# Two parts of the FFN's Down as seven half-width products, with the next part's first features ahead of them

## The chip, the cores and the metric

The kernel runs on one core of a Trainium2 chip. The time is device time in microseconds (us) of one execution. TensorE (PE in the profile; its weight loads are PEld) multiplies, VectorE (DVE), ScalarE (ACT) and GpSimd (POOL) work on tiles, and SyncE (SP) issues DMA transfers; POOL and ACT can issue transfers too. PE writes to PSUM, eight banks of 128 x 512 float32; the other tiles lie in SBUF, 128 partitions wide.

## The reference

A two-layer trunk over 512 positions and 1024 features. Each layer is

```python
x = x + 0.5 * swiglu(rms_norm(x, ffn1_norm[l]), ffn1_w_gate[l], ffn1_w_up[l], ffn1_w_down[l])
...     # mixer: causal convolution beside differential attention with a relative-position bias
x = x + jnp.concatenate([conv_out, diff_out], axis=-1) @ w_out[l]
x = x + 0.5 * swiglu(rms_norm(x, ffn2_norm[l]), ffn2_w_gate[l], ffn2_w_up[l], ffn2_w_down[l])

def swiglu(h, w_gate, w_up, w_down):
    return (jax.nn.silu(h @ w_gate) * (h @ w_up)) @ w_down
```

with 2816 hidden features in each FFN, all in float32. There are four FFNs in all, two in each layer, and they are most of the time.

## The kernel before, in words

**Layout.** Features are on the partitions and positions along the free dimension: `x` is eight tiles of 128 x 512. The 2816 hidden features are 22 feature tiles. Every float32 operand is split in a high part (ACT, a copy to float32r) and a low part (DVE, the difference), by `parts_of` (L95 to L97) for weights and by other lines for activations; `mm3` (L160 to L166) multiplies with three matmuls: high x high, high x low, low x high.

**One FFN** (`ffn`, from L382) goes through its 22 feature tiles in three parts, (0 to 5), (6 to 13), (14 to 21). For each part it makes the gated features, and then adds the part's share of the Down product to `x`.

- Part one is plain: per feature tile, Gate and Up each take 8 input tiles x 3 matmuls of 512 columns. The first two feature tiles go through `first_products`, beside which the row norm is worked out (`rows_rstd`, `spread`). At the start of the kernel the weights of the first tile, `lead`, are loaded in halves.
- From tile 6 on, Gate and Up of one feature tile are made together by `seven`: the two outputs, the two halves of the contraction and the two halves of the columns form a 2 x 2 by 2 x 2 block product, which takes seven block products in place of eight. Each is 4 input tiles x 3 matmuls of 256 columns, so a feature tile takes 84 of them. Its activations are sums and differences of the normalised input, made once per FFN by `Halves` and put in place by `settle`. Its weights are sums of blocks, made for each feature tile by `sums` (L123): SP loads the raw tiles, POOL issues one transfer that adds onto a loaded tile (L140), POOL adds twice (L145, L146), and ACT and DVE split the results. `rest`, the last of the seven products and the gating, is carried out inside the next tile's `seven`, by `finish`.
- Down is plain in all three parts (L429 to L444): for each of the eight outputs as many feature tiles as the part has, 3 matmuls of 512 each into `ps_d`, weights by `gather` in chunks of eight blocks; DVE then adds half the sum to `x` (L442). After the last part, `after(m)` prepares `x` tile m for the next stage (`Prep.tile`), or writes it out.

**Buffers.** Raw, high and low weight tiles lie in rings: `wraw` has five slots of 1024 columns, `whi` and `wlo` four, the half-size rings two. A transfer waits until its slot has been read for the last time. PSUM banks rotate in three pairs (`turn_tag`, `pair_banks`).

**Order.** The program is traced once; a planner then fixes the order of the instructions on each engine ahead of time, by priority in program order and its own model of times. Each engine and each DMA queue works its list in that order, so whatever stands behind a waiting instruction waits too. Matmuls marked `keep_in_program_order` are not moved against each other: here the first matmul of each of the seven products.

**The mixer** adds the position bias to the scores in `softmaxes` (L681). The bias table, 128 x 4 x 512, is made once by `make_bias` during the first FFN and kept in SBUF (`bias`, loaded by POOL's queue).

## Time and profile before

| | |
|---|---|
| median of three runs | 1805.25 us (1803.75 to 1805.65) |
| the profiled execution | 1805.29 us, span 1803.5 us |
| granted TensorE clock | full (1.0) |
| PE busy, matmuls | 1786.9 us, 10692 |
| DVE, ACT, POOL busy | 1207.3, 884.2, 616.7 us |
| matmuls of `seven` (L352), 256 columns | 5376 |
| matmuls of Down (`ps_d`), 512 columns | 2112 |
| DMA | 227 MB, 126 GB/s over the span |

How to read the lines of the profile: a group of instructions stands with its line in the kernel, its engine, the operation and output<-input. In the chain that ended last each line is the start in us, the time in us and what ran. In the timeline each line is the start, the time from there to the end, and the instruction; what stands in brackets is the engine's idle time before it and what ended that. SPq is SP's DMA queue. Matmuls are pipelined: one of 512 columns shows 0.39 us, while the next starts 0.23 us after it.

### The profile page before, as it was taken

The page shows a single profiled execution, that of the slowest core. Times are in us where ns is not written, and L with a number is a line of the kernel's source. Part 1 is how long each engine was busy: PE and PEld are TensorE (multiplying, and loading weights), DVE is VectorE, ACT ScalarE, POOL GpSimd, SP SyncE. Part 2 cuts the span into 40 slices and gives each one's busy share as a digit, 9 for nine tenths or more (in the row PEclk, how much of TensorE's full clock was granted, in tenths as well). Part 3 has the DMA queues.
Part 4 walks back from the last instruction along what each step waited for, and adds up shares of the span by engine and source line. Part 5 has one row for each costly group of instructions (what it writes and reads, how often), then busy time and mean ns, then how long its engine had stood idle before and what let it go on. Part 6 is the DMA issues. An engine that isn't in the chain of part 4 may idle for free.

```text
span 1803.5 us, 27857 instructions
## 1 busy us (share of the span) xinstructions
PE 1786.9 (99%) x10692; PEld 1584.1 (88%) x10692; DVE 1207.3 (67%) x1852; ACT 884.2 (49%) x1448; POOL 616.7 (34%) x432
## 2 busy tenths in 40 slices
PE   8999999999999999999999999999999999999999
PEld 6799899888778889899888998998887888998997
DVE  7857557568867857557576684665788587574662
ACT  5536346445854436346434462554558354463551
POOL 3035123269942024133110341322797320231320
PEclk9999999999999999999999999999999999999999
DMA  6357456322212347546433474653231133574561
GB/s 219 125 149 197 135 144 179 115 89 90 75 41 88 107 116 183 155 126 182 126 93 103 127 201 108 167 172 106 71 107 57 47 103 97 146 178 133 154 171 51
DMA packets 104853, 227.00 MB, mean 126 GB/s; under 512 B 11527, under 2 KB 29094, under 8 KB 104720
## 3 DMA queue, kind: packets, MB, share of 16 engines
q1 hardware_dynamic: 85536, 188.78, 32.3%
q0 software_dynamic: 19040, 36.36, 11.7%
q8 instruction: 83, 1.36, 0.3%
q14 instruction: 50, 0.41, 0.1%
q10 hardware_dynamic: 144, 0.08, 0.0%
HBM read 223.07 MB, written 3.42 MB: 126 GB/s over the span
## 4 chain that ended last, share of the span: by engine, by line
PE 95%; DVE 2%; ACT 1%; issue 1%; DMA 0%; SPq 0%; ACTq 0%; DVEq 0%
PE ps_pair L352 36%; PE ps_d L166 9%; PE ps_d L162 9%; PE ps_d L165 9%; PE ps_pair L166 6%; PE ps_pair L165 6%; PE ps_pair L162 6%; PE ps_pair L559 2%; PE ps_pair L560 2%; PE ps_pair L561 2%; PE ps_out L165 1%; PE ps_out L162 1%; PE ps_sc L677 1%; PE ps_out L166 1%; DVE actl L248 1%; PE ps_v L591 1%
## 5 line engine op out<-in xcount | busy, mean ns | idle before, releaser
L96 ACT ACTIVATE whi<-wraw 128x1024 fp32r<-128x1024 f32 (+1 forms) x578 | 459.0, 817 | 648.9 <-PE ps_d L165 226.1
L97 DVE TENSOR_TENSOR wlo<-wraw,whi 128x512 fp32r<-128x512 f32 (+1 forms) x534 | 513.6, 984 | 184.1 <-ACT whi L96 179.2
L352 PE MATMUL ps_pair<-acth,wlo 128*128 128x256 f32 x1024 | 289.8, 283 | 0.0
L352 PE MATMUL ps_pair<-actl,whi 128*128 128x256 f32 x1024 | 289.8, 283 | 0.0
L352 PE MATMUL ps_pair<-acth,whi 128*128 128x256 f32 x1024 | 289.7, 283 | 0.0
L165 PE MATMUL ps_d<-hl,whi 128*128 128x512 f32 x704 | 274.0, 389 | 0.0
L166 PE MATMUL ps_d<-hh,wlo 128*128 128x512 f32 x704 | 272.7, 389 | 0.0
L162 PE MATMUL ps_d<-hh,whi 128*128 128x512 f32 x704 | 268.9, 389 | 0.0
L140 POOL DMA_DIRECT2D wraw<-in_gu x64 | 77.2, 1207 | 452.6 <-DMA wraw<-in_gu 210.8
L352 PE MATMUL ps_pair<-th,wlo 128*128 128x256 f32 x768 | 217.3, 283 | 0.0
L352 PE MATMUL ps_pair<-tl,whi 128*128 128x256 f32 x768 | 217.2, 283 | 0.0
L352 PE MATMUL ps_pair<-th,whi 128*128 128x256 f32 x768 | 217.2, 283 | 0.0
L162 PE MATMUL ps_pair<-acth,whi 128*128 128x512 f32 x512 | 200.6, 395 | 5.5 <-ACT whi L96 5.5
L165 PE MATMUL ps_pair<-actl,whi 128*128 128x512 f32 x512 | 201.1, 393 | 2.0 <-DVE actl L248 1.6
L166 PE MATMUL ps_pair<-acth,wlo 128*128 128x512 f32 x512 | 200.5, 392 | 0.6 <-DVE wlo L97 0.6
L442 DVE SCALAR_TENSOR_TENSOR x<-ps_d,x 128x512 f32<-128x512 f32 x96 | 65.0, 689 | 197.3 <-PE ps_d L166 197.3
L352 PEld LDWEIGHTS ps_pair<-acth,whi 128*128 128x128 f32 x1024 | 196.6, 192 | 0.3
L352 PEld LDWEIGHTS ps_pair<-actl,whi 128*128 128x128 f32 x1024 | 196.6, 192 | 0.3
L352 PEld LDWEIGHTS ps_pair<-acth,wlo 128*128 128x128 f32 x1024 | 196.6, 192 | 0.0
L145 POOL TENSOR_TENSOR wraw<-wraw 128x512 f32<-128x512 f32 x64 | 87.8, 1373 | 304.3 <-DMA wraw<-in_gu 220.1
L165 PEld LDWEIGHTS ps_d<-hl,whi 128*128 128x128 f32 x704 | 132.2, 188 | 27.0
L166 PEld LDWEIGHTS ps_d<-hh,wlo 128*128 128x128 f32 x704 | 132.2, 188 | 27.0
(174 smaller groups left out, 3306.4 us busy)
## 6 DMA issues: line engine op xcount, KB each, us to landing
wraw<-in_gu SPq DMA_DIRECT2D x110, 512.0 KB, 3.6
wraw<-in_gu SPq DMA_DIRECT2D x196, 256.0 KB, 3.9
wraw<-in_gu POOLq DMA_DIRECT2D x64, 512.0 KB, 5.6
wraw<-in_wqkv SPq DMA_DIRECT2D x24, 512.0 KB, 3.5
wraw<-in_dn SPq DMA_DIRECT2D x52, 192.0 KB, 3.0
wraw<-in_wag SPq DMA_DIRECT2D x16, 512.0 KB, 3.5
wraw<-in_wout SPq DMA_DIRECT2D x16, 512.0 KB, 3.5
wraw<-in_dn SPq DMA_DIRECT2D x24, 320.0 KB, 3.4
```

The lines of the kernel that those rows point to most:

```text
L96: S.activation(hi, raw, AF.Copy)
L97: (eng or V).tensor_tensor(out=lo, in0=raw, in1=f32(hi), op=ALU.subtract)
L140: nc.gpsimd.dma_start(two.rearrange("p (b c) -> p b c", b=2), u[:, h[0]].unsqueeze(1).broadcast_to([P, 2, 512]), accum_op=ALU.add)
L145: G.tensor_tensor(more[:, h[0]], two[:, h[1]], whole[:, h[0]], op=ALU.add)
L162: first = T.matmul(ps, wh, xh, start=start, stop=False)
L165: T.matmul(ps, wh, xl, start=False, stop=False)
L166: T.matmul(ps, wl, xh, start=False, stop=stop)
L352: mm = T.matmul(ps, l, r, start=first and i == j == 0, stop=False, skip_group_check=True)
L442: V.scalar_tensor_tensor(x[:, m, :], ps, 0.5, x[:, m, :], op0=ALU.mult, op1=ALU.add)
L559: T.matmul(ps[n], xh[:, t], wh, start=k == 0, stop=False)
L560: T.matmul(ps[n], xh[:, t], wl, start=False, stop=False)
L561: T.matmul(ps[n], xl[:, t], wh, start=False, stop=k == KT - 1)
```

## The change

**Parts.** There are now four parts, of 6, 6, 6 and 4 feature tiles. The first and the last are as before (class `Kept`: plain Down). The two in the middle are `Paired`: their Down is made by `seven` too, for two outputs at a time, with the contraction of six tiles in two halves of three, and the columns in two halves. The class makes the sums and differences of two gated tiles, `kk` and `kk + 3`, as soon as both are there, so its features are made in the order 0, 3, 1, 4, 2, 5. The weights come from `sums`, now with blocks of 384 columns (`n`) and with sources that can lie across two stored chunks (`blocks_of`), in which case a load is two transfers. What follows the products is in the new classes `Gate` (for Gate and Up, as before but for `second`) and `Update` (for Down: it adds to `x`, with one addition on POOL, `kept`).

**Order.** After a paired part's last feature, the first feature of the next part is put ahead of the Down products. `late` now runs on from features to Down and on into the next part.

**Start.** The weights of the first two feature tiles are loaded and split in halves, all first halves ahead of the second ones, with the `x` tiles between; `lead_products` runs the two tiles' Gate and Up side by side over the input tiles, and the norm's `spread` moves into the third tile's second product.

**Bias.** `make_bias` stops at the copy in DRAM; each mixer loads the table from there through SP's queue into its own memory. Some scratch tiles (`make_scalars`, `Halves`) use other buffers.

```diff
-PARTS = ((0, 6), (6, 8), (14, 8))
+PARTS = (
+    ((0, 1, 2, 3, 4, 11), False), (tuple(range(5, 11)), True), (tuple(range(12, 18)), True), (tuple(range(18, 22)), False),
+)
...
+    def blocks_of(src, half, b0):
+        def get(a, b):
+            got, at = [], a
+            while at < b:
+                n, c = divmod(b0 * P + at, 1024)
+                w = min(b - at, 1024 - c)
+                got.append((at - a, at - a + w, src[half, n][:, c : c + w]))
+                at += w
+            return got
+        return get
...
+        load(whole[:, both], g, 0)
         two = ring("wraw")
+        load(two[:, h[0]], g, 0)
+        load(two[:, h[1]], u, n)
+        u2 = ring("wraw2", 512)[:, :n]
+        load(u2, u, n)
+        for c0, c1, ap in u(0, n):
+            nc.gpsimd.dma_start(
+                two[:, both].rearrange("p (b c) -> p b c", b=2)[:, :, c0:c1],
+                ap.unsqueeze(1).broadcast_to([P, 2, c1 - c0]), accum_op=ALU.add,
+            )
...
-    nc.scalar.dma_start(pars[0], par[0])
-    nc.sync.dma_start(x[:, 0, :], xt[0])
-    lead = [chunk(gu1[0, 0, i], cuts=2) for i in range(2)]
-    for k in range(1, KT):
-        nc.sync.dma_start(x[:, k, :], xt[k])
-    nc.gpsimd.dma_start(pars[1], par[1])
+    for l in range(DEPTH):
+        nc.scalar.dma_start(pars[l], par[l])
+    lead = [[ring("wraw"), ring("whi"), ring("wlo")] for _ in range(4)]
+    for half in range(2):
+        h, kk = slice(half * 512, (half + 1) * 512), range(half * KT // 2, (half + 1) * KT // 2)
+        nc.sync.dma_start(x[:, kk[0], :], xt[kk[0]])
+        for n, (raw, hi, lo) in enumerate(lead):
+            nc.sync.dma_start(raw[:, h], gu1[0, n // 2, n % 2][:, h])
+            parts_of(raw[:, h], hi[:, h], lo[:, h])
+        for k in kk[1:]:
+            nc.sync.dma_start(x[:, k, :], xt[k])
...
+    def lead_products(pr, w, ps):
+        for k in range(KT):
+            for n in range(2):
+                for i in range(2):
+                    mm3(ps[n][i], wpart(w[n][i], k), pr[k], k == 0, k == KT - 1)
+        return rows_rstd(pr.s, DM, pin=True)[0]
...
+    class Paired:
+        BLOCKS = {"b11": 0, "t1": 1, "t2": 2, "t3": 3, "t4": 4, "b21": 5, "b22": 6}
+        def __init__(self, fp, many, ahead):
+            self.fp, self.half = fp, many // 2
+            self.made, self.t = {}, {}
+            self.order = [kk + n for kk in range(self.half) for n in (0, self.half)]
+        def place(self, kk, bank):
+            if kk >= self.half:
+                return bank
+            self.t[kk] = self.fp.tile([P, 5, HS], F32, tag="ht", name="ht")
+            return self.t[kk][:, :2].rearrange("p n c -> p (n c)")
+        def took(self, kk, us):
+            if kk < self.half:
+                return
+            kk -= self.half
+            t = self.t[kk]
+            us = us.rearrange("p (n c) -> p n c", n=2)
+            hi, lo = (self.fp.tile([P, 7, HS], F32R, tag=f"hw{n}", name="hw") for n in (kk, self.half + kk))
+            S.activation(hi[:, 5:], us, AF.Copy)
+            V.tensor_tensor(t[:, 3], us[:, 1], t[:, 1], op=ALU.subtract)
+            V.tensor_tensor(t[:, 1], t[:, 0], t[:, 1], op=ALU.subtract)
+            V.scalar_tensor_tensor(t[:, 2], us[:, 1], -1.0, t[:, 1], op0=ALU.mult, op1=ALU.subtract)
+            V.scalar_tensor_tensor(t[:, 4], us[:, 0], -1.0, t[:, 2], op0=ALU.mult, op1=ALU.subtract)
+            S.activation(hi[:, :5], t, AF.Copy)
+            V.tensor_tensor(lo[:, 5:], us, f32(hi[:, 5:]), op=ALU.subtract)
+            V.tensor_tensor(lo[:, :5], t, f32(hi[:, :5]), op=ALU.subtract)
+            self.made[kk] = hi, lo
...
+    class Gate:
+        scale = 1.0
...
+        def first(self, two, keep):
+            V.tensor_tensor(two, two, keep[:, 0::2], op=ALU.add)
+            S.activation(keep[:, 0::2], two, AF.Silu)
+        def second(self, a, keep, bank):
+            V.tensor_tensor(keep[:, 1::2], a, keep[:, 1::2], op=ALU.add)
+            us = self.part.place(self.kk, bank)
+            V.scalar_tensor_tensor(
+                us.rearrange("p (n c) -> p n c", n=2), keep[:, 1::2], -1.0, keep[:, 0::2], op0=ALU.mult, op1=ALU.mult
+            )
+            self.part.took(self.kk, us)
+    class Update:
+        scale = -0.5
+        def __init__(self, m):
+            self.x = [x[:, m + i].rearrange("p (n c) -> p n c", n=2) for i in range(2)]
+        def kept(self, keep):
+            G.tensor_tensor(self.x[1], self.x[1], keep[:, 1::2], op=ALU.add)
+        def first(self, two, keep):
+            V.scalar_tensor_tensor(keep[:, 0::2], two, 0.5, keep[:, 0::2], op0=ALU.mult, op1=ALU.subtract)
+            V.tensor_tensor(self.x[0], self.x[0], keep[:, 0::2], op=ALU.add)
+        def second(self, a, keep, bank):
+            V.scalar_tensor_tensor(self.x[1], a, -0.5, self.x[1], op0=ALU.mult, op1=ALU.add)
...
+                if paired:
+                    if n + 1 < len(PARTS):
+                        pair(n + 1, 0, False)
+                    half, f0 = divmod(fs[0], HALF)
+                    for m in range(0, KT, 2):
+                        g, u = (blocks_of(dn, half, (m + i) * HALF + f0) for i in range(2))
+                        w = sums(g, u, part.half * P)
+                        end = n + 1 == len(PARTS) and m + 2 == KT
+                        late.append(seven(part, part.half, w, pair_banks(next(turn)), fp, finish, end, Update(m)))
...
-        skew = bass.AP(d2.tensor, d2.offset + P - 1, [[RLEN - 1, P], [P * RLEN, HEADS], [1, SEQ]])
-        nc.gpsimd.dma_start(bias, skew)
+        skew.append(bass.AP(d2.tensor, d2.offset + P - 1, [[RLEN - 1, P], [P * RLEN, HEADS], [1, SEQ]]))
...
+            bias = mp.tile([P, HEADS, SEQ], F32, tag="bias", name="bias")
+            nc.sync.dma_start(bias, skew[0])
+            row["bias"] = bias
```

## The prediction

> **What bounds the kernel now.** First the page: busy time by engine, and the chain that ended last.

> ```profile
> PE 1786.9 (99%) x10692; PEld 1584.1 (88%) x10692; DVE 1207.3 (67%) x1852; ACT 884.2 (49%) x1448; POOL 616.7 (34%) x432
> ...
> PE 95%; DVE 2%; ACT 1%; issue 1%; DMA 0%; SPq 0%; ACTq 0%; DVEq 0%
> ```

> TensorE is the bound, but overlapping matmuls make 99% say nothing of their pace. That is read from the chain in order of time:

> ```profile
> 20.06 0.50 PE ps_pair L165
> 21.71 2.25 DVE wlo L97
> 24.00 0.50 PE ps_pair L166
> ...
> 92.28 0.68 PE ps_d L162 x3
> 113.59 76.31 PE ps_pair L352 x636
> ```

> A 512-column matmul takes 0.68 / 3 = 0.2267 us, a 256-column one 76.31 / 636 = 0.1200 us. From 24 us on each FFN is gapless at these two paces, so fewer columns on PE is time, if the weights keep coming. How near they come to being late is in the timeline of one gate/up pair (seven x 12 matmuls, 10.08 us; this one begins at 142.2 us):

> ```profile
> 140.58 1.21 POOL L140 DMA_DIRECT2D wraw<-in_gu  x1
> 146.39 1.30 POOL L145 TENSOR_TENSOR wraw<-wraw 128x512 f32<-128x512 f32 x1 [4.61 <-DMA wraw<-in_gu]
> 147.77 2.33 POOL L146 TENSOR_TENSOR wraw<-wraw 128x512 f32<-128x512 f32 x1
> 151.17 1.20 POOL L140 DMA_DIRECT2D wraw<-in_gu  x1 [1.07 <-DVE wlo L97]
> ...
> 144.72 0.42 SPq L136 DMA_DIRECT2D wraw<-in_gu  x1
> ...
> 147.71 1.23 DVE L97 TENSOR_TENSOR wlo<-wraw,whi 128x1024 fp32r<-128x1024 f32 x1
> ...
> 149.50 1.16 ACT L96 ACTIVATE whi<-wraw 128x512 fp32r<-128x512 f32 x2 [0.72 <-PE ps_pair L352]
> ```

> POOL issues the adding transfer, waits until it has landed (5.8 us from issue), adds twice (3.7 us), and only then issues the next: a round of 9.5 us in a period of 10.08. The sums are there at 146.39 and ACT takes them at 149.50, so they are about 3.1 us ahead (2.6 to 3.1 in this stage). The POOL add beside a DVE split took 2.33 us, an undisturbed one 1.30 (at 101.38 us).

> **The sum is made against** the profiled execution, 1805.29 us (span 1803.5, 1.8 around it), 0.04 from the median of the three runs, 1805.25.

> **Products, -19.2 us.** Of the 22 feature tiles of an FFN, 12 get their Down as seven products. For two outputs and six tiles, 2 x 6 x 3 = 36 matmuls of 512 (8.16 us) become 7 x 3 x 3 = 63 of 256 (7.56 us): 0.60 saved. Four output pairs, two parts, four FFNs: 32 x 0.60 = 19.2. Gate and Up keep their counts (six plain pairs, sixteen by seven). The pace of 0.1200 holds with a fresh weight load per matmul, so the added loads are in it.

> **Start, -4 us.** The first matmul begins at 5.53 us; the six plain pairs end at 80.73. Going back from there, four pairs are 192 x 0.2267 = 43.5 us and the bias and spread matmuls between them 1.9, so two pairs and the row sums end at 35.3. Gapless from 5.53 they would end at 5.53 + 96 x 0.2267 + 0.35 = 27.6: 7.6 us are lost, because a feature tile gives PE 6 matmuls (1.36 us) while ACT needs 0.71 + 0.62 for it and DVE 1.1 to 1.6. With both pairs interleaved a tile gives 12 (2.72 us), longer than either. What stays: four first halves must be in place for the first tile. The first transfers come in at 8.04 (ACT's wait), ACT then needs some 0.6 for each, so the first 12 matmuls end near 10.2 instead of 8.25: 2 us. The lead also holds all four slots of whi and wlo, and the third pair's chunk is split (1.06 + 1.3) only behind a first output with nine matmuls left (2.0): about 0.5. Gain 7.6 - 2.5 = 5; I take 4, since DVE shares those microseconds with POOL's row sums. Bounds: -5.5, and +1 if the third pair waits for a whole split. The late normaliser (spread in the third pair's second product) is ready about 4 us after the row sums, used after 7.5; three pairs to gate at once instead of two keep DVE, already full from 40 to 60 us, as late as before.

> **Weights of the down sums, +7 us.** Each output pair replaces gathers by five or six SP transfers (0.33 to 0.49 us each), one or two POOL transfers (1.2 each; two in two of eight), two POOL adds of 384, six splits of 384 to 768 columns, three DVE updates at 0.69 where there were two, and POOL's `kept` add (1.3, as POOL's tap additions of that size, L631). DVE: splits 0.87 + 5 x 0.5, updates 2.1: 5.4 of 7.56. ACT about 4.6. Neither is full alone. POOL's round: landing between 5.0 (three quarters of the data) and 5.8, adds 2.0 to 2.7 (three quarters of 1.3 + 1.3 and of 1.3 + 2.3): 7.0 to 8.5, against 7.56, if `kept` runs inside the wait for the landing. Near 7.9, the rounds of three down sums fall behind by about 0.35 each, and that of the first gate sum after them by 1.0: 1.7 to 2, covered by the 3.1 in hand. What isn't covered is a second transfer (1.2, in one sum of each part) and POOL and DVE in each other's way. I take 0.9 for each of the eight parts. Bounds: 0 and 4.5 per part (the first rival).

> [...]

> **Other edges, +1 us.** Gating a pair of features costs DVE four 256-wide operations (0.42), a split of 1280 (1.5) and one of 512 where there were two of 512: +1.2 per feature in 10.08, on 7.2 to 8.2 busy of 10; ACT +0.4. Hidden by the products. `second` is one 0.69 for two of 0.43. The first feature of the next part runs ahead of the Down and covers the last gating (second rival). The last Down has four tiles, 2.72 us for an output instead of 5.44, and per output DVE needs 0.69 + 0.75 + half a 1.23 split, ACT 0.71 + 0.62 + 0.53: both fit, so a late tile costs at most 1 us in each of three handovers; +1. The bias (1 MB) moves from POOL's queue to SP's and is loaded twice; its cover is the start of the mixer, from 367 to the first scores at 464.65 us, and only if SP stood behind another wait would it be late: 0, bounds 0 and +5 each. The Halves' buffers and the other first-block transfers move nothing on PE: 0, bounds -0.5 and +1.

> Sum: 1805.3 - 19.2 - 4 + 7 + 1 = **1790**.

> **Rivals.** First, on the other side: **POOL's round becomes the pace.** POOL works in order, and `kept` waits for PE's third product of the running pair. If it stands between the adds and the next transfer instead of inside the landing wait, a round is 7.9 + 1.4 = 9.3 us; three rounds of down sums and the first gate sum are then late by about 1.75 + 4 x 1.4 - 2.8 = 4.5 us per part, 36 in all: 1805.3 - 23 + 36 + 1 = 1819. It decides at 23 / 8 = 2.9 us per part. For it: the round had 0.6 us to spare in a longer period. Against: POOL idles 4.3 to 5.7 us of each round, in which `kept` fits. With half of it 1801.

> Second, **the way into the Down waits.** After the last feature's product (4.32 us into the pair run ahead) come 0.69 + 0.69 + 1.7 + 1.3 + 1.5 = 5.9 us of gating, and up to 3.9 of weight splits on DVE: the third tile is ready 10.2 to 14.1 us in, wanted at 10.8. Only if PE's fixed order runs other products' first two tiles meanwhile (some 36 matmuls, 4.3 us) is it free. Half of it, 1.6 x 8 = 13: 1803. Against: the order before already interleaves `ps_d` with the pairs and leaves no gap there.

> Third, **the start gains nothing** because all weights must now come first; with the rest as forecast, 1794.

> **Chances.** Forecast 0.48 (own range 1781 to 1798, the start's and the weights' bounds); POOL's round 0.26 (1799 to 1825); way into the Down 0.18 (1794 to 1808); start 0.08 (1790 to 1799). To leave out two in ten: low 1780 (19.2 and 5.5 and nothing lost), high 1815, which keeps most of POOL's rival. Faster by over 0.2% (3.6 us, about what a measurement of this kernel can tell from no change): 0.48 + 0.08 + 0.10 of the way in + 0.04 of POOL's round = 0.70; within it 0.06; slower 0.24, nearly all POOL's.

> **What would show it.** The products: 63 matmuls in 7.56 us in each output pair, and PE's line for the sevens near 7392 matmuls. The start: pairs one and two done near 31 us. The weights: POOL's adds on down sums ahead of ACT's split by over 0.5 us; wrong if splits follow the landing at once and PE's weight loads wait for ACT or DVE at the last down pairs and the first pairs after them. The way in: no wait of PE's for `hw` at the first down product. The bias: landed before the first scores. The forecast is wrong on its sign if each part loses 2.9 us or more.

## The result, and the profile after

The changed kernel takes 1901.21 us (median of 4 runs, 1892.62 to 1907.3) against 1805.34 for the kernel before on the same chip: 1.0532 times as long, with an interval from 1.0512 to 1.0552. The forecast was 1790, between 1780 and 1815; the sign is wrong and the time lies far outside. The profiled execution took 1901.78 us, its span is 1900.0, the granted clock 0.982.

The page of the changed kernel, its first part (busy time), the row of the granted clock, and the first line of the chain:

```profile
PE 1813.0 (95%) x11556; PEld 1642.0 (86%) x11556; DVE 1459.2 (77%) x2094; ACT 992.0 (52%) x1688; POOL 791.8 (42%) x566
...
PEclk9999899999999999899999999989999999998999
...
PE 39%; DVE 7%; DMA 7%; POOL 3%; issue 3%; ACT 1%; POOLq 0%; DVEq 0%; ACTq 0%; SPq 0%
```

Before, the chain was 95% PE. Now DVE, DMA and POOL appear in it (its shares add up to 60%, because it could be followed back only to 774 us), and the clock has dips in slices that were full before. What PE waits for, over the whole changed kernel (total us, times, longest), says which tiles are late:

```profile
PE ps_pair L468 <- ACT whi L97: 33.6, 16, 3.4
PE ps_pair L468 <- DVE wlo L98: 17.8, 28, 2.3
PE ps_pair L468 <- DVE hw L445: 9.1, 8, 1.1
PE ps_pair L185 <- ACT whi L97: 7.5, 2, 6.1
PE ps_rows L236 <- POOL ssum L286: 6.0, 2, 3.0
PE ps_pair L468 <- ACT hw L443: 2.6, 5, 0.9
```

The first two lines are weights of the seven products that are not split yet (51.4 us). Lines three and six are the way into the Down (11.7). The fifth is the handover to the next stage. The fourth is the start, where PE waits before its first matmul in both kernels.

Where the time went, by stage. For each stretch of one kind of matmul I took its length in the PE timeline and subtracted matmuls x 0.2267 (512 columns) or x 0.1200 (256). The entry into a paired Down, with its wait for `hw`, is counted with the Gate and Up stage before it; the first matmuls of the next feature, which run between the last down products, are counted with the Down:

| | before | after |
|---|---|---|
| six plain pairs at the start end at | 80.8 us | 79.2 us |
| lost in the Gate and Up stages by seven products | 0 | 36.6 |
| lost in the eight paired Downs | (plain) 0 | 70.2: 10.0, 11.6, 10.1, 7.5, 6.4, 10.0, 12.1, 2.5 |
| lost in the first stage of the two mixers | 3.9 | 12.2 |
| lost at the start of the second layer | 0.3 | 1.6 |

1803.5 - 19.2 (fewer columns) - 1.6 + 36.6 + 70.2 + 8.3 + 1.3 = 1899.1, against a span of 1900.0.

**How one part loses its time.** This is POOL's timeline in the first paired part of the changed kernel. L160 issues the adding transfer, L166 and L167 are the two adds, L524 is `kept`; in brackets stands POOL's idle time before. The first two lines are DVE's and SP's: a split, and the three loads that the transfer at 189.69 waits for.

```profile
183.24 1.84 DVE L98 TENSOR_TENSOR wlo<-wraw,whi 128x384 fp32r<-128x384 f32 x2
185.11 1.28 SPq L145 DMA_DIRECT2D wraw<-in_dn  x3
...
189.69 1.20 POOL L160 DMA_DIRECT2D wraw<-in_dn  x1 [3.73 <-DVE wlo L98]
190.45 1.78 POOL L524 TENSOR_TENSOR x<-x,keep 128x512 f32<-128x512 f32 x1
194.90 1.01 POOL L166 TENSOR_TENSOR wraw<-wraw 128x384 f32<-128x384 f32 x1 [2.67 <-DMA wraw<-in_dn]
195.99 1.62 POOL L167 TENSOR_TENSOR wraw<-wraw 128x384 f32<-128x384 f32 x1
197.57 1.61 POOL L524 TENSOR_TENSOR x<-x,keep 128x512 f32<-128x512 f32 x1
199.30 1.20 POOL L160 DMA_DIRECT2D wraw<-in_dn  x1
206.72 0.99 POOL L166 TENSOR_TENSOR wraw<-wraw 128x384 f32<-128x384 f32 x1 [6.22 <-issue]
207.79 1.21 POOL L167 TENSOR_TENSOR wraw<-wraw 128x384 f32<-128x384 f32 x1
208.97 1.59 POOL L524 TENSOR_TENSOR x<-x,keep 128x512 f32<-128x512 f32 x1
210.51 1.20 POOL L160 DMA_DIRECT2D wraw<-in_gu  x1
219.49 1.26 POOL L166 TENSOR_TENSOR wraw<-wraw 128x512 f32<-128x512 f32 x1 [7.78 <-DMA wraw<-in_gu]
```

Three things add up. At 189.69 the transfer is late (POOL idles 3.73 us) because the loads of its tile could start only when a split had freed the slot: the split ends at 185.08, the loads are issued from 185.11 on, and by the trace the last of them landed at 189.13. The bracket names another split, which happened to end at that moment; of the 32 down sums' first transfers in this kernel 25 start 0.5 to 0.6 us after the last load of their tile has landed. Then `kept` stands between the adds and the next transfer (at 197.57 and 208.97, 1.6 us each, and again at 222.39). At 210.51 and 224.07 the transfer follows right behind it. The one at 199.30 it did not hold up: that tile's last load landed at 198.74, 0.56 us before. And the later transfers take longer from issue to first add: 5.2 us for the one at 189.69, then 7.4 and 9.0. From add to add a round is 11.8 and 12.8 us, where an output pair on PE lasts 7.56. The same pattern stands in the later parts (the fourth transfer of the next paired part takes 8.7 us, the two after it 9.8 and 8.3).

ACT's timeline shows that the splits now follow the landing at once, with ACT idle before them:

```profile
206.66 0.52 ACT L97 ACTIVATE whi<-wraw 128x384 fp32r<-128x384 f32 x1 [3.43 <-DMA wraw<-in_dn]
...
219.41 0.63 ACT L97 ACTIVATE whi<-wraw 128x512 fp32r<-128x512 f32 x1 [4.76 <-DMA wraw<-in_gu]
```

And PE pays twice: once for the wait, and once more because it comes back at half pace. Its timeline:

```profile
207.24 0.50 PE L468 MATMUL ps_pair<-hw,whi 128*128 128x256 f32 x2 [1.40 <-ACT whi L97]
208.19 0.39 PE L468 MATMUL ps_pair<-hw,wlo 128*128 128x256 f32 x1 [0.45 <-DVE wlo L98]
...
220.09 0.58 PE L468 MATMUL ps_pair<-acth,whi 128*128 128x256 f32 x1 [2.84 <-ACT whi L97]
...
221.73 0.41 PE L468 MATMUL ps_pair<-acth,whi 128*128 128x256 f32 x1
221.94 0.41 PE L468 MATMUL ps_pair<-actl,whi 128*128 128x256 f32 x1
...
226.00 0.41 PE L468 MATMUL ps_pair<-th,wlo 128*128 128x256 f32 x1
```

From 221.73 to 226.00 the starts lie 0.213 us apart instead of 0.120. In the table by stretches of the same kernel the last figures are the granted clock, the DMA share and GB/s:

```profile
209.00:212.70 3.70, 3.70 (x21) 3.70 (x20) 3.49 (x6) 2.11 (x5) 2.70 (x3) 0.54 0.29 37
...
220.00:226.20 6.20, 5.64 (x24) 5.35 (x25) 5.80 (x6) 2.48 (x6) 5.19 (x4) 0.50 0.14 14
```

The clock was 0.54 and 0.50 in these. Over the span 0.982 means that 0.018 x 1900 = 34 us of full-speed time are missing, but a part of that fell into waits, in which it cost nothing. The matmuls of L468 that started at half pace lost about 24 us, between a fifth and a quarter of the 106.8; in the kernel before they lose nothing.

### The profile page after: what moved, and what is told of

Same layout as the page of the kernel before. It is cut to its first block, busy times and chain, and to the rows that moved or that the text cites. A ratio compares the mean times of both kernels' runs of the same rounds, so it can differ in the third digit from the quotient of the medians.

```text
span 1900.0 us, 30891 instructions
## 1 busy us (share of the span) xinstructions
PE 1813.0 (95%) x11556; PEld 1642.0 (86%) x11556; DVE 1459.2 (77%) x2094; ACT 992.0 (52%) x1688; POOL 791.8 (42%) x566
## 4 chain that ended last, share of the span: by engine, by line
PE 39%; DVE 7%; DMA 7%; POOL 3%; issue 3%; ACT 1%; POOLq 0%; DVEq 0%; ACTq 0%; SPq 0%
PE ps_pair L468 18%; DMA wraw<-in_gu 5%; DVE wlo L98 4%; PE ps_pair L188 3%; PE ps_pair L189 3%; PE ps_pair L185 3%; PE ps_d L185 2%; PE ps_d L189 2%; PE ps_d L188 2%; DMA wraw<-in_dn 2%; DVE actl L278 1%; POOL x L524 1%; POOL wraw L166 1%; POOL wraw L167 1%; PE ps_pair L743 1%
## 5 line engine op out<-in xcount | busy, mean ns | idle before, releaser
L97 ACT ACTIVATE whi<-wraw 128x1024 fp32r<-128x1024 f32 (+3 forms) x724 | 516.2, 734 | 623.8 <-PE ps_pair L468 196.3
L98 DVE TENSOR_TENSOR wlo<-wraw,whi 128x512 fp32r<-128x512 f32 (+3 forms) x680 | 663.5, 996 | 192.1 <-ACT whi L97 185.1
L166 POOL TENSOR_TENSOR wraw<-wraw 128x512 f32<-128x512 f32 (+1 forms) x96 | 132.0, 1375 | 470.9 <-DMA wraw<-in_gu 287.1
L468 PE MATMUL ps_pair<-acth,whi 128*128 128x256 f32 x1024 | 294.0, 287 | 23.3 <-ACT whi L97 23.3
L468 PE MATMUL ps_pair<-acth,wlo 128*128 128x256 f32 x1024 | 297.1, 290 | 11.1 <-DVE wlo L98 10.6
L468 PE MATMUL ps_pair<-actl,whi 128*128 128x256 f32 x1024 | 292.8, 286 | 0.0
L468 PE MATMUL ps_pair<-hw,whi 128*128 128x256 f32 x1344 | 256.4, 291 | 22.1 <-ACT whi L97 10.3
L468 PEld LDWEIGHTS ps_pair<-hw,whi 128*128 128x128 f32 x1344 | 217.9, 199 | 26.3 <-ACT whi L97 11.4
L468 PEld LDWEIGHTS ps_pair<-acth,whi 128*128 128x128 f32 x1024 | 199.4, 195 | 25.7 <-ACT whi L97 25.5
L468 PE MATMUL ps_pair<-th,whi 128*128 128x256 f32 x768 | 221.5, 288 | 0.0
L468 PE MATMUL ps_pair<-tl,whi 128*128 128x256 f32 x768 | 221.4, 288 | 0.0
L468 PE MATMUL ps_pair<-th,wlo 128*128 128x256 f32 x768 | 220.9, 288 | 0.0
L468 PEld LDWEIGHTS ps_pair<-acth,wlo 128*128 128x128 f32 x1024 | 199.8, 195 | 17.0 <-DVE wlo L98 16.6
L468 PE MATMUL ps_pair<-hw,wlo 128*128 128x256 f32 x672 | 195.6, 291 | 7.3 <-DVE wlo L98 7.1
L468 PEld LDWEIGHTS ps_pair<-actl,whi 128*128 128x128 f32 x1024 | 199.5, 195 | 0.2
L160 POOL DMA_DIRECT2D wraw<-in_gu x64 | 77.1, 1205 | 275.4 <-DVE actl L370 177.5
L468 PEld LDWEIGHTS ps_pair<-tl,whi 128*128 128x128 f32 x768 | 151.8, 198 | 0.3
L468 PEld LDWEIGHTS ps_pair<-th,whi 128*128 128x128 f32 x768 | 151.8, 198 | 0.3
L468 PEld LDWEIGHTS ps_pair<-th,wlo 128*128 128x128 f32 x768 | 151.7, 197 | 0.0
```

The costliest lines, as they stand in the source:

```text
L97: S.activation(hi, raw, AF.Copy)
L98: (eng or V).tensor_tensor(out=lo, in0=raw, in1=f32(hi), op=ALU.subtract)
L160: nc.gpsimd.dma_start(two[:, both].rearrange("p (b c) -> p b c", b=2)[:, :, c0:c1], ap.unsqueeze(1).broadcast_to([P, 2, c1 - c0]), accum_o ...
L166: G.tensor_tensor(more[:, h[0]], two[:, h[1]], whole[:, h[0]], op=ALU.add)
L468: mm = T.matmul(ps, l, r, start=first and i == j == 0, stop=False, skip_group_check=True)
```

## The experiments

Each kernel was run beside the kernel before on the same chip (1804.5 to 1804.8 us). All are single runs except where an interval is given. The changed kernel itself spreads by 15 us over its four runs, so differences of a few microseconds between single runs carry nothing.

### Is it the paired Down at all?

```diff
-    ((0, 1, 2, 3, 4, 11), False), (tuple(range(5, 11)), True), (tuple(range(12, 18)), True), (tuple(range(18, 22)), False),
+    ((0, 1, 2, 3, 4, 11), False), (tuple(range(5, 11)), False), (tuple(range(12, 18)), False), (tuple(range(18, 22)), False),
```

> All four parts with a plain Down, the rest of the change kept. If the seven-product Down and what it does to the weights of its neighbours is the whole loss (70 us in the Down stages, 37 us in the pairs between them), PE has no gaps there and the time is 1805.3 - 1.6 (start, as the changed kernel shows it) + 8.3 (longer way into the two mixers and the second layer) + 1 = about 1813. If the smaller parts, the bias or the start cost more than that, it is over 1825.

Measured: 1813.94 us. The four parts, the new start and the bias are kept, only the Down is plain. The Gate and Up stages and the Downs lose under 1 us in all. So the loss of about 107 us in these stages comes with the paired Down, also that in the Gate and Up stages next to it. What stays, some 9 us, is in the handovers (below).

### `kept` on POOL

The first kernel leaves out the addition of `keep` to the second output's `x`, and so shows only time; the second makes it on DVE.

```diff
-            G.tensor_tensor(self.x[1], self.x[1], keep[:, 1::2], op=ALU.add)
+            pass
```

> The addition on POOL of a down pair's first product to x is left out (the result lacks that term), nothing else. If POOL's round is the pace and this addition, 1.6 to 1.8 us, lies in it, four late rounds in each of eight parts get shorter by 1.7: 54 us less, about 1847. If the landing of the adding transfer sets the pace and the addition only fills its wait: under 15 us less, 1887 or more.

```diff
-            G.tensor_tensor(self.x[1], self.x[1], keep[:, 1::2], op=ALU.add)
+            V.tensor_tensor(self.x[1], self.x[1], keep[:, 1::2], op=ALU.add)
```

> The same addition made by DVE (0.69 us) in place of POOL. POOL's round as the pace: about 1850, as without it, if DVE has room. DVE as the bound: no better than now, about 1900. Landing as the pace: 1887 or more.

Measured: 1876.46 without it, 1860.34 with it on DVE. The Downs lose 45.4 and 42.4 us instead of 70.2. So taking `kept` off POOL, where it is 32 x 1.73 = 55 us of work, made the whole 25 to 41 us shorter: it is a part of the cause, and it isn't all. Both times lie between the two that were expected. With it on DVE, the fourth transfer of the first paired part starts no earlier (199.94) and still took 7.4 us to its first add, and the first gate transfer 8.5. That the kernel with less work is the slower one of the two isn't explained; the 16 us between them are little more than the 15 by which four runs of one kernel spread, and the planner orders each kernel anew.

### The adding transfer

For the down sums POOL makes four adds in place of the transfer and two adds; `u` comes whole through SP. For room the scratch of `spread` shares a buffer.

```diff
-        load(two[:, h[0]], g, 0)
-        load(two[:, h[1]], u, n)
...
+        if n < 512:
+            uu = ring("wraw2", 768)
+            load(uu, u, 0)
+            u2 = uu[:, n:]
+            G.tensor_tensor(two[:, h[1]], u2, uu[:, :n], op=ALU.add)
+            G.tensor_tensor(two[:, h[0]], whole[:, h[0]], uu[:, :n], op=ALU.add)
...
-            dg = tmp.tile([P, NT, P], dt, tag=("diag", "sq")[n], name="diag", bufs=1 + n)
+            dg = tmp.tile([P, NT, P], dt, tag="sq", name="diag", bufs=2)
```

> For the down sums alone the adding transfer is gone: Up's counterpart is loaded whole by SP, and POOL makes four additions of 384 columns in place of two; POOL then waits for no transfer that it issued itself. If landing inside POOL's order is the pace, the Down stages lose under 3 us each in place of 8.8 and the time is 1840 to 1855. If POOL and DVE hold each other up (additions 1.0 to 1.8 us each, four of them and the one to x: 6 to 8.5 us in 7.56), little changes: 1880 to 1910.

Measured: 1951.36, worse than either theory. The Downs lose 53.7 us and the Gate and Up stages 78.2. It tells nothing sure of the transfer: the mixers' attention stages, which have no down sums, take 23 us longer as well, so the shared scratch has a price of its own, and how much of the rest is due to it can't be told.

### The order in which a sum's tiles are loaded

The ring `wraw` has five slots and a sum takes three, `whole`, `two`, `more`. The transfer adds onto `two`. As `two` was second, it took the slot that `more`, two sums earlier, left, and that is split late. The edit puts it first, where by the ring's order it follows `whole` of two sums earlier, and it also puts its loads first in SP's order:

```diff
-        whole = ring("wraw")
-        load(whole[:, both], g, 0)
         two = ring("wraw")
         load(two[:, h[0]], g, 0)
         load(two[:, h[1]], u, n)
+        whole = ring("wraw")
+        load(whole[:, both], g, 0)
```

> In the sums the tile that the adding transfer works on is taken from the ring and loaded ahead of the whole block, in place of behind it: two lines change places. It then takes the slot of a tile that is split about 5 us earlier. If the adding transfer is late because its tile comes late, and only then runs into the next loads, the Down stages lose under 3 us each (now 8.8) and the pairs between them under 2 (now 3): 1815 to 1835. If POOL's order is the cause by itself (landing, two additions, the one to x, in a row), nothing changes: 1890 to 1905.

The same with `kept` on DVE:

> The same, with the addition to x on DVE. Both causes together: 1800 to 1815, that is the 19 us of the products less 9.5 at the handovers and what is left. POOL's order alone: as with the addition on DVE only, 1860.

Measured: 1840.46 and 1827.79, 5 and 13 us above the ranges that were expected. Moving these lines gives 61 us of the 96; with `kept` on DVE 73. The Downs then lose 25.7 and 13.1 us, the Gate and Up stages 19.0 in both, about half of it the wait for `hw` on DVE (9.9 and 10.5). POOL's timeline in the same part, order changed and `kept` on DVE:

```profile
189.02 1.20 POOL L160 DMA_DIRECT2D wraw<-in_dn  x1 [4.39 <-DVE keep L509]
194.44 1.01 POOL L166 TENSOR_TENSOR wraw<-wraw 128x384 f32<-128x384 f32 x1 [4.22 <-DMA wraw<-in_dn]
...
198.53 1.20 POOL L160 DMA_DIRECT2D wraw<-in_dn  x1 [1.65 <-DMA wraw<-in_dn]
203.74 1.02 POOL L166 TENSOR_TENSOR wraw<-wraw 128x384 f32<-128x384 f32 x1 [4.00 <-DVE wlo L98]
...
206.46 1.21 POOL L160 DMA_DIRECT2D wraw<-in_gu  x1
212.95 1.44 POOL L166 TENSOR_TENSOR wraw<-wraw 128x512 f32<-128x512 f32 x1 [5.28 <-DMA wraw<-in_gu]
```

The transfers take 5.4, 5.2 and 6.5 us now, not 5.2, 7.4 and 9.0, and from 190 to 235 us PE's longest wait is 1.1 us. The tables by stretches show what had happened to the DMA engines. The changed kernel (last: clock, DMA share, GB/s):

```profile
207.00:211.00 4.00, 3.31 (x19) 3.11 (x20) 3.44 (x4) 2.19 (x6) 3.92 (x4) 0.77 0.16 60
...
220.00:227.00 7.00, 6.45 (x31) 6.15 (x32) 6.30 (x7) 3.11 (x7) 5.19 (x4) 0.55 0.17 27
```

and the same stretches with the order changed and `kept` on DVE:

```profile
207.00:211.00 4.00, 4.00 (x36) 4.00 (x35) 3.62 (x8) 2.31 (x6) 0.67 (x1) 1.00 0.77 125
...
220.00:227.00 7.00, 7.00 (x61) 7.00 (x60) 4.91 (x5) 3.66 (x7) 5.14 (x3) 1.00 0.69 215
```

In the changed kernel the DMA engines stood at 16 and 17% while POOL added and ACT and DVE split; between these stretches (211 to 220 us) they were at 83%, with the adding transfer among the loads of the next sum. My reading is a loop: slot, load, adding transfer, adds, split, slot. A longer turn of it bunches the loads, and the transfers that share the bunch come late.

That the order of the tiles decides is shown; whether by the slot or by the place in SP's order is not, since the edit changes both. In the part above the tile's loads start no earlier (185.08 for 185.11), and the transfer 0.7 us. What differs is the bunch. Counted over the changed kernel, a transfer beside which three or more loads of raw weights were issued, from 0.5 us before it to 2 us after, took a median of 8.1 us to land (512 KB, 14 of them) or 7.4 (384 KB or parts of it, 6); one beside which there was none took 5.6 or 5.0 (30 and 31). With the order alone changed a single transfer had such company. The busy share of the DMA engines wasn't the difference: from 199 to 207 us it was 0.78 in the changed kernel, where the transfer at 199.30 took 7.4 us to its first add, and 0.88 with the new order and `kept` on DVE, where the one at 198.53 took 5.2. So in the changed kernel late landings went with loads issued close by; no run changed this alone.

Would another slot do the same?

```diff
-    RING = {"wraw": 5, "whi": 4, "wlo": 4, "wraw2": 2, "whi2": 2, "wlo2": 2}
+    RING = {"wraw": 6, "whi": 4, "wlo": 4, "wraw2": 2, "whi2": 2, "wlo2": 2}
```

(with `two` in its old place, `kept` on DVE, and the shared scratch for room)

> A sixth slot of raw weights (room made by sharing one scratch tile of the norm's spread and by dropping a spacer), with the addition to x on DVE. The tile of the adding transfer then takes the slot of the same tile two sums before, which is split at the same point as now: if it is this slot that counts, the Down stages lose as much as with the addition on DVE alone (5.3 each), apart from the mixers, which the shared scratch tile may slow. If it is room in the ring at large, under 2 each.

Measured: 1920.55. The Downs lose 39.5 us, against 42.4 with five slots, the Gate and Up stages 58.1 against 21.4, and the attention stages take 25 us longer, as in the other kernel with the shared scratch. So a sixth slot bought next to nothing in the Downs; what it does elsewhere can't be told from what the scratch does.

### The start and the bias alone

Three parts of 6, 8 and 8, all plain, with the rest of the change:

```diff
-    ((0, 1, 2, 3, 4, 11), False), (tuple(range(5, 11)), True), (tuple(range(12, 18)), True), (tuple(range(18, 22)), False),
+    (tuple(range(6)), False), (tuple(range(6, 14)), False), (tuple(range(14, 22)), False),
```

> Three parts of 6, 8 and 8 with a plain Down as before the change; only the start, the bias through SP and the moved scratch tiles of the change remain. If the longer handovers come from the last part of four tiles, they are as before (mixers' first stage loses 2 us, not 5 to 7), and the time is before less the start's 1.3 to 1.6: ratio 0.999. If they come from the bias or the scratch tiles, it is 7 to 9 us slower: 1.004 to 1.005.

Measured: 1804.64, ratio 1.0003, interval 0.9993 to 1.0013 (10 runs). In its trace the plain pairs end at 79.15 us, 1.6 earlier than before, and the mixers' first stages lose 2.2 and 2.1 us, as before the change (2.1 and 1.8). So start and bias together are worth nothing that can be measured, and the longer handovers come with the last part of four.

### The way into the Down, and the shape of the parts

On top of the changed order and `kept` on DVE, the larger half of the low parts goes first:

```diff
-            V.tensor_tensor(lo[:, 5:], us, f32(hi[:, 5:]), op=ALU.subtract)
             V.tensor_tensor(lo[:, :5], t, f32(hi[:, :5]), op=ALU.subtract)
+            V.tensor_tensor(lo[:, 5:], us, f32(hi[:, 5:]), op=ALU.subtract)
```

> As the version with the adding transfer's tile first and the addition to x on DVE (1827.8), and in the making of the paired tiles the low part of the five combined blocks (1.5 us on DVE) goes ahead of that of the two plain ones (0.7): two lines change places. The first down product waits 1.4 us for it in each part (10.5 us in all). If DVE's order is what delays it, each wait gets 0.6 to 0.7 shorter: 5 to 6 us, 1822. If ACT's high part ends last, nothing changes: 1828.

Measured: 1827.73, no change; PE's wait for `hw` on DVE is 10.0 us over eight Downs, against 10.5. The trace of this run shows why: DVE still makes the smaller half first, at 181.37, and starts the larger only when ACT's high part is there, after 0.74 us of idling:

```profile
182.79 1.49 DVE L444 TENSOR_TENSOR hw<-ht,hw 128x1280 fp32r<-128x1280 f32 x1 [0.74 <-ACT hw L443]
```

Then the parts themselves: four features first and six last (the making of the halves' activations moves one feature forward),

```diff
+    ((0, 1, 2, 3), False), (tuple(range(4, 10)), True), (tuple(range(11, 17)), True), ((10, 17, 18, 19, 20, 21), False),
```

> The same, with parts of 4 plain, 6 paired, 6 paired and 6 plain (two more features by seven products: 2 x 0.8 x 4 = 6.4 us off PE). If the longer handovers (mixers' first stages 5 to 7 us of loss in place of 2, the second layer 1.6 in place of 0.3) come from the four-tile last part, they fall back by most of 9.5 us, to 2 to 4: 1808 to 1814. If DVE does not get through the normalised halves in a first part of four, the first pairs of the second part wait: 1820 or more.

or four features as a paired part:

```diff
+    (tuple(range(6)), False), (tuple(range(11, 17)), True), ((6, 7, 8, 9), True), ((10, 17, 18, 19, 20, 21), False),
```

> Six plain features first, a paired part of six, a paired part of four (two tiles in each half, weights of 256 columns), six plain last. Products saved: 5/6 of 19.2 = 16. Handovers as with six tiles last. The period of a down pair of the four-tile part is 5.04 us, shorter than POOL's round (5 + 1.7 + 1.2): if that round is what paces the Down, this part loses more than the six-tile one, 4 to 8 us each time, 1815 to 1830; if the tile's early load hides it, 1810.

Measured: six last 1822.89, ratio 1.0098, interval 1.0079 to 1.0117 (4 runs); four paired 1866.62, above both times expected, where each paired part of four loses 9 to 11 us. With six features last the mixers' first stages lose 2.2 and 2.0 us again and the wait for `ssum` is gone from PE's waits. So the handovers are explained, but the time is above the 1808 to 1814 that this was to bring: the Downs and the Gate and Up stages lose 9 us more than with the parts as they were, and why is open. What it was is seen in the changed kernel. DVE, then POOL, then PE at the end of the first FFN:

```profile
375.02 2.48 DVE L627 SCALAR_TENSOR_TENSOR x<-ps_d,x 128x512 f32<-128x512 f32 x4 [3.38 <-PE ps_d L189]
...
393.35 1.32 POOL L286 TENSOR_TENSOR ssum<-ssum,sq 128x512 f32<-128x512 f32 x1 [0.88 <-ACT sq L285]
394.73 0.66 PE L236 MATMUL ps_rows<-ident,ssum 128*128 128x128 f32 x4 [2.98 <-POOL ssum L286]
```

Four outputs finish together once the last feature is gated, and only then does the next stage's work on `x` begin. With eight features in the last part (the kernel of the start alone) the updates come one at a time, 5.44 us apart:

```profile
355.10 0.69 DVE L627 SCALAR_TENSOR_TENSOR x<-ps_d,x 128x512 f32<-128x512 f32 x1 [2.69 <-PE ps_d L189]
360.54 0.69 DVE L627 SCALAR_TENSOR_TENSOR x<-ps_d,x 128x512 f32<-128x512 f32 x1 [2.69 <-PE ps_d L189]
```

Six features last is the best version of the paired Down that was run, still 1% slower than the kernel before. In it the Downs lose 18.4 us and the Gate and Up stages 22.5, together over 5 us for each paired part that saves 2.4; 11.5 of the 41 are the wait for `hw`.

## Why the prediction was wrong, step by step

**Products, -19.2: right.** The matmuls of line L468 are 7392. Where weights are there, the pace holds: 33 matmuls from 213.02 to 216.97 us, 0.1197 each.

**Weights of the down sums, +7: the step that failed.** They cost some 95 us, the 106.8 of the two kinds of stages less the 11.7 of the way in, where 7 were allowed; 106.8 is 13.4 per part, and the sign was to turn at 2.9. I set POOL's round at 7.0 to 8.5 us and its excess against the 3.1 us in hand. The adds were priced right: 2.2 to 2.6 against 2.0 to 2.7. POOL's work did not fill its rounds: in those of 11.8 and 12.8 us it stood idle for 6.22 and 7.78. Wrong were three things. `kept` was assumed to run inside the landing wait; in the first paired part it does so once and stands between the adds and the next transfer three times, twice holding it up, and it takes 1.73 us (median), not 1.3. The landing was taken as fixed, 5.0 to 5.8; to the first add it grew to 9.0 where loads were issued close by. And the wait for a slot, ahead of the 3.73 us that POOL idles before one transfer, had no term at all: I counted queue times and never asked which earlier tile frees the slot of the tile that the transfer adds onto. The 3.1 us in hand were also counted from the landed tile; the first sum that POOL makes of it is ready 1.3 us later (146.39 + 1.30).

**First rival, POOL's round as the pace: the right place, a part of the mechanism, a third of the size.** It said 4.5 us per part and 1819. The rounds of the first paired part were 9.0 to 12.8 us, not 9.3, and the Downs alone lost 8.8 us per part. Taking `kept` out of POOL's way gave 25 to 41 us, the order of the tiles 61. A rival with one fixed round had no term for landings that differ, from issue to first add 5.2 to 9.0 us in that part.

**The granted clock: no term.** The forecast priced a microsecond of waiting as a microsecond. After 13 of the 16 waits of 1.4 us and more inside these stages PE ran at half pace, for 3 to 7 us each; the matmuls lost about 24 us by it in all.

**Second rival, the way into the Down: true beside the first.** It said 1.6 us per part. PE waits for `hw` in all eight Downs, 9.1 + 2.6 = 11.7 us or 1.5 per part.

**Start, -4: mis-sized, -1.6.** The step took 0.2267 us for every matmul from the first on. The changed kernel's PE timeline shows otherwise:

```profile
9.76 0.63 PE L189 MATMUL ps_pair<-acth,wlo 128*128 128x512 f32 x1
10.18 0.63 PE L185 MATMUL ps_pair<-acth,whi 128*128 128x512 f32 x1
...
14.02 0.63 PE L189 MATMUL ps_pair<-acth,wlo 128*128 128x512 f32 x1
14.45 0.48 PE L185 MATMUL ps_pair<-acth,whi 128*128 128x512 f32 x1
```

Until 14.45 us the starts are 0.43 apart. From 8.74 on these are 13 matmuls, 13 x (0.43 - 0.2267) = 2.6 us that the new order did not win back. The kernel before has the same pace there, from 9.92 to 13.06 us, so this could have been read. The first matmul also starts 0.5 us later (6.07 for 5.53). In place of "near 31 us" the row sums stand at 32.95. And of the 1.6 us nothing is left in the time of the run with the start and the bias alone.

**Other edges, +1: handovers +9.6.** "Both fit" was worked out for outputs 2.72 us apart; the four first outputs come at once, because the last feature's gating holds all of them. The bias was right: the attention stages take as long as before.

## What to carry to other kernels

A stage whose weights go through slot, load, transfer, add and split is a loop, and its turn must be worked out with the slot's release in it: for each tile, which earlier tile frees its slot and when. When the spare time of such a loop falls from 0.6 us to below nothing, price a wait of PE at more than its length: here the fall of the clock made about 24 of the 106.8 us, and by my reading the bunched loads added to the waits. Price also small work on the queue that issues the loop's transfers: `kept`, 1.73 us on POOL 32 times, was worth 25 to 41 us.

## What the runs showed of the hardware that was not expected

**The granted clock fell after short waits of PE.** After waits of 1.40 + 0.45 us (207 to 208 us) and of 2.84 us (220.09) the 256-column matmuls started 0.213 us apart in place of 0.120, for 3.2 and 4.9 us, and the granted clock over these stretches was 0.54 and 0.50. Waits of 1.14 us were, with one exception, not followed by it. The longest of these waits was 3.4 us and the shortest that was followed by it 1.1.

At the start the column of the granted clock says 1.00 while the matmuls are 0.43 apart; the record begins only at 14.63 us, where the pace changes, so before that the pace must be read from the starts.

**The adding transfers' times differed within one kernel.** The same 512 KB took a median of 5.8 us from issue to landing over the kernel, and 9.0 and 8.2 to the first add in the two issues at 210.51 and 224.07; 384 KB took 5.2 and 7.4. With three or more loads issued close by, the medians to landing were 8.1 and 7.4 us, without any 5.6 and 5.0.
